# Differential attention on one core: heads that take turns, and band attention's output kept by token halves

## The chip, the cores and the metric

The kernel runs on one core of a Trainium2 chip. The metric is the device time of one execution in microseconds (us), the median of several runs. Engines are called PE (TensorE, the matrix engine; PEld is its weight load), DVE (VectorE), ACT (ScalarE), POOL (GpSimd) and SP (SyncE, which here only issues DMAs). Lnnn is a line of the kernel file before the change.

## The reference

One layer over 1024 tokens of width 1024, in float32: a SwiGLU feed-forward half step, two attentions in parallel whose gated outputs are added, and a second feed-forward half step. The part around the change, cut short:

```python
a = chunked_band_attention(qa, ka, va, rel_table)        # 8 heads of 64, band of 576 keys
b = diff_attention(qb, kb, vb, t5_table, lam, ...)       # 4 heads, see below
x = x + (sigmoid(g_a) * (a @ w_branch_a) + sigmoid(g_b) * (b @ w_branch_b)) @ w_o

# diff_attention, for a head h and a query block of 128 tokens (8 blocks):
sc   = q[r] @ k[r].T * scale + bias[h]                   # r = 0, 1: two score maps, d = 64
p    = softmax(where(allowed, sc, NEG))                  # keys up to the query's chunk
o    = (p[0] - lam * p[1]) @ v                           # v is 128 wide
y    = rms_norm(o, subln_g) * (1 - lambda_init)
```

Query block i sees the keys of blocks 0 to i, so block 0 has 128 keys and block 7 has 1024.

## The kernel before

Every product in float32 is made of three TensorE products of parts: a tensor is split into a rounded part (`whi`, cast on ACT, L96) and the remainder (`wlo`, subtracted on DVE, L101), and `mm3` issues hi·hi, lo·hi and hi·lo (L127, L128, L129).

The program runs through stages one after the other. By the timeline these are the first feed-forward block (to about 690 us), the norm and the projection into queries, keys, values and gates (to about 1112), band attention (to about 1225), differential attention (to about 1402), the gated sum with w_o (to about 1570) and the second feed-forward block. The change lies in band attention and in differential attention.

Both attentions are written as generators ("jobs"). `run(jobs)` keeps up to four jobs live and advances them in turn, the new one first. A job of differential attention, `jobs_b(hb, filler)`, is one query block of one head: it makes the two score maps on PE (`sc`, two PSUM banks), adds the bias `nb` and takes the minimum on DVE (L692, `pm`), takes the exponential on ACT (L694) and combines the two maps on DVE (L829). Then it rests for a turn. Then come the transposes of the probabilities on PE (L700, `pt`), split again on ACT and DVE (`whi`, `wlo`), the products with the values (L845 and L846, `pv`), the norm (`o`, `sq`, `dg`) and the final product `try` (L860), which is split into the output tile `y`. The jobs of a head run in the order of blocks 0 to 7, heads one after another.

With the first job of a head its operands are loaded from DRAM: six half tiles `qs`, `ks`, `kl` of 512 KB each (L123), two halves of 64 partitions apiece, and the values `vt` of 1024 KB. The bias `nb` (L705, two DMAs of 512 KB) serves two heads, so that it is loaded for the first and for the third head. Heads 0 to 3 of differential attention are called the first to the fourth here; their loads are `q4` to `q7` in the order below. A change of head is called a switch: switch 1 is from the first to the second head.

Between these jobs the kernel does a piece of other work, `branch_a`, in 16 filler steps: band attention's output times w_branch_a. A filler step reads a tile of gates `g` (`gl`), makes 12 matmuls into `pb`, multiplies on DVE (L794) and stores the result with a DMA on SP (`ta`, L795). After each block `due[0] += 0.5` says that half a step is due. One weight chunk `wa` (512 KB, L118, a single buffer) serves four filler steps, and each of its two column blocks is split once for two steps.

Nothing but the tile pools holds the loads back. The large tiles (8 KB per partition: `qs`, `ks`, `kl`, `vt`, `y`, `nb`) share the tag "big" with 14 buffers; units of split data have WU = 18 buffers, temporary tiles (`gl`, `o1`, `o2`, `sq` and others) TF = 10. The order of the instructions on each engine is set when the kernel is compiled, by a scheduler that works from the program order and from these pools. Each engine runs its instructions in that order, and all the DMAs named here are issued by SP in order: what waits on SP holds back what stands behind it.

Of the kernel before, what the change touches and what calls it, by code (L numbers as in the profile page):

```python
# [9 lines left out]
F32 = mybir.dt.float32  # L10
# [6 lines left out]
P = 128  # L17
S = 1024
D = 1024
NT = S // P  # L20
KT = D // P
HALF = 512
# [22 lines left out]
RAW, WU, TF, TT = 6, 18, 10, 3  # L45
# [8 lines left out]
def hybrid_layer_kernel(ctx, tc, x, ffn1_norm, ffn1_w_in, ffn1_w_out, mix_norm, w_mix_in,  # L54
# [13 lines left out]
    def big(shape, name, dtype=F32R):  # L68
        return sb.tile(shape, dtype, tag="big", bufs=14, name=name)
# [47 lines left out]
    def load(src, tile_):  # L117
        nc.sync.dma_start(out=tile_, in_=src)  # L118
        return tile_
# [535 lines left out]
    ys = []  # L655
    with tc.tile_pool(name="ps2", bufs=1, space=PSUM) as ps:
# [64 lines left out]
        def jobs_a(pr):  # L721
            ctx_ = {}

            def job(sb_, h):
                if not ctx_:
                    ctx_["qkv"] = load_qkv(pr)
                    ctx_["y"] = big([P, 2, S], "y")
                    ys.append(ctx_["y"])
                    ctx_["nb"] = big([P, 2, S], "nb", F32)
                    for hh in range(2):  # L730
                        bias_rows(ctx_["nb"][:, hh, :WA], diag_a, 2 * pr + hh, EA, WA)
                qkv, y, nb = (ctx_[n] for n in ("qkv", "y", "nb"))
# [66 lines left out]
        def jobs_b(hb, filler):  # L799
            ctx_ = {}  # L800

            def job(i):
                if not ctx_:
                    ctx_["qkv"] = load_qkv(4 + hb)
                    ctx_["y"] = big([P, 2, S], "y")
                    ys.append(ctx_["y"])
# [29 lines left out]
                due[0] += 0.5  # L836
# [32 lines left out]
        due = [0]  # L869
        for hb in range(4):  # L870
            jobs += jobs_b(hb, filler)
# [5 lines left out]
    with tc.tile_pool(name="ps3", bufs=1, space=PSUM) as ps:  # L877
# [7 lines left out]
        for jj in range(KT // 2):  # L885
            wr = load(w_cols(w_branch_b[0], jj * 256, 256, 0, 4), raw_tile([P, 4, 256]))
            for j in (2 * jj, 2 * jj + 1):
                w = split_units(wr[:, :, (j % 2) * P:(j % 2 + 1) * P], branch_unit)
                for g in range(2):
# [3 lines left out]
                    for k in range(4):  # L893
                        mm3(pb, [v[:, k, :] for v in w], [cols(ys[4 + k][:, v, :], g) for v in range(2)],
                            k == 0, k == 3)
# [83 lines left out]
```

## Time and profile before

| | |
|---|---|
| median of 3 runs | 2207.89 us (2207.6 to 2208.07) |
| profiled execution | 2210.82 us, its span 2209.0 us, mean PE clock 0.979 |
| PE busy in the span | 2100.4 us (95%) |
| DVE busy | 1448.2 us (66%) |
| ACT busy | 991.2 us (45%) |
| POOL busy | 286.4 us (13%) |
| differential attention, 1225 to 1402 us | PE 151.73 of 177, DVE 137.50, ACT 107.72 |

The profile has one execution. In a table by windows each row gives a stretch of time, its length, and the busy time of PE, PEld, DVE, ACT and POOL with the count of instructions in brackets; then the PE clock that was granted (1.00 is full), the mean busy share of the DMA engines and their rate in GB/s. In a timeline a row has the start, the duration, the engine, the line and what is written from what; a bracket at its end gives the idle time before it and what ended that.

### The profile page before, as it was taken

The numbers are of one execution on the slowest core, as the hardware profiler recorded it, in microseconds if no ns is written. First come the engines' busy times: TensorE is split into PE (matmuls) and PEld (weight loads), VectorE is DVE, ScalarE is ACT, GpSimd is POOL, SyncE is SP. The second block draws the span as 40 slices with busy tenths as digits, with TensorE's granted clock in tenths as the row PEclk, the third lists the DMA queues.
The fourth block names the chain that finished last, engine by engine and source line by source line (L and its number), as shares of the span: only waits on it lengthen the run. The fifth ranks groups of instructions, "written<-read, shape, count | busy, mean of one in ns | idle before, by whom it ended". The sixth has DMA issues, their size and how long they took to land. (4 is left out here: it accounts for less than half of the span.)

```text
span 2209.0 us, 29778 instructions
## 1 busy us (share of the span) xinstructions
PE 2100.4 (95%) x10373; PEld 1779.8 (81%) x10373; DVE 1448.2 (66%) x2620; ACT 991.2 (45%) x1972; POOL 286.4 (13%) x371
## 2 busy tenths in 40 slices
PE   5999999999997999999999988899799999999997
PEld 4888888888886998888878877788688888888886
DVE  8765656577567756655378877658756565658566
ACT  5433333334445444444478756335433333334444
POOL 6130000000006100000056333104300000000000
PEclk8999999999998999999999989999999999999999
DMA  4374323284353445542497555755423232367335
GB/s 136 100 198 115 119 83 118 96 305 162 115 154 112 134 154 171 172 148 91 120 226 184 125 152 139 225 166 172 119 86 120 88 116 93 111 224 240 97 115 186
DMA packets 262246, 319.72 MB, mean 145 GB/s; under 512 B 16732, under 2 KB 162156, under 8 KB 262096
## 3 DMA queue, kind: packets, MB, share of 16 engines
q1 hardware_dynamic: 257888, 309.91, 45.3%
q0 software_dynamic: 4064, 7.39, 1.5%
q8 instruction: 82, 1.34, 0.3%
q14 instruction: 68, 0.56, 0.1%
q10 hardware_dynamic: 144, 0.52, 0.1%
HBM read 219.44 MB, written 98.30 MB: 144 GB/s over the span
## 5 line engine op out<-in xcount | busy, mean ns | idle before, releaser
L101 DVE TENSOR_TENSOR wlo<-raw,whi 128x512 fp32r<-128x512 f32 x197 | 141.6, 719 | 183.3 <-PE prod L128 109.7
L96 ACT CAST whi<-raw 128x512 fp32r<-128x512 f32 x200 | 124.4, 622 | 273.8 <-PE prod L128 224.5
L96 ACT CAST whi<-T 128x512 fp32r<-128x512 f32 x192 | 119.5, 623 | 282.7 <-PE prod L128 163.0
L128 PE MATMUL po<-wlo,whi 128*128 128x512 f32 x616 | 240.0, 390 | 0.0
L129 PE MATMUL po<-whi,wlo 128*128 128x512 f32 x616 | 239.9, 390 | 0.0
L127 PE MATMUL po<-whi 128*128 128x512 f32 x616 | 236.4, 390 | 0.0
L101 DVE TENSOR_TENSOR wlo<-T,whi 128x512 fp32r<-128x512 f32 x189 | 134.2, 710 | 98.3 <-ACT whi L96 74.4
L112 DVE TENSOR_TENSOR c<-prod,c 128x512 f32<-128x512 f32 (+1 forms) x201 | 133.2, 664 | 99.7 <-PE prod L129 98.7
L101 DVE TENSOR_TENSOR wlo<-B,whi 128x512 fp32r<-128x512 f32 x154 | 107.0, 695 | 129.2 <-ACT whi L96 129.2
L96 ACT CAST whi<-B 128x512 fp32r<-128x512 f32 x154 | 95.7, 622 | 206.9 <-PE po L128 185.3
L138 POOL TENSOR_TENSOR r<-v,neg_half 128x1 f32<-128x1 f32 x64 | 44.3, 693 | 758.9 <-DVE v L155 721.2
L129 PEld LDWEIGHTS po<-whi,wlo 128*128 128x128 f32 x616 | 115.7, 188 | 24.1
L127 PEld LDWEIGHTS po<-whi 128*128 128x128 f32 x616 | 115.7, 188 | 23.9
L128 PEld LDWEIGHTS po<-wlo,whi 128*128 128x128 f32 x616 | 115.7, 188 | 23.8
L184 POOL TENSOR_TENSOR xt<-xt,gain 128x512 f32<-128x512 f32 x36 | 49.1, 1380 | 516.4 <-DMA xt<-xm 484.3
L96 ACT CAST whi<-ha 128x512 fp32r<-128x512 f32 x154 | 94.8, 616 | 39.0 <-PE prod L128 17.2
L101 DVE TENSOR_TENSOR wlo<-ha,whi 128x512 fp32r<-128x512 f32 x154 | 105.7, 687 | 10.0 <-ACT whi L96 10.0
L258 ACT COPY c<-prod 128x512 f32<-128x512 f32 (+1 forms) x201 | 103.3, 573 | 5.2 <-issue 2.6
L694 ACT ACTIVATE pm<-pm,mn 128x640 f32<-128x640 f32 (+7 forms) x128 | 94.1, 736 | 17.4 <-DVE mn L692 16.1
L127 PE MATMUL prod<-S1h,whi 128*128 128x512 f32 (+1 forms) x252 | 96.5, 383 | 2.2 <-ACT S1h L96 2.2
L127 PE MATMUL prod<-S4h,whi 128*128 128x512 f32 (+1 forms) x252 | 96.1, 381 | 1.8 <-ACT c L258 1.8
L127 PE MATMUL prod<-A11h,whi 128*128 128x512 f32 (+1 forms) x252 | 96.8, 384 | 0.7 <-ACT A11h L96 0.7
(247 smaller groups left out, 5835.4 us busy)
## 6 DMA issues: line engine op xcount, KB each, us to landing
raw<-in_ffn_w_in_dram SPq DMA_DIRECT2D x88, 512.0 KB, 3.9
ha<-hS SPq DMA_DIRECT2D x88, 256.0 KB, 2.7
raw<-in_w_mix_in_dram SPq DMA_DIRECT2D x40, 512.0 KB, 4.1
ha<-hA SPq DMA_DIRECT2D x66, 256.0 KB, 2.7
hA<-c SPq DMA_DIRECT2D x64, 256.0 KB, 2.5
B<-in_ffn_w_out_dram SPq DMA_DIRECT2D x12, 1024.0 KB, 5.9
hS<-hs SPq DMA_DIRECT2D x44, 256.0 KB, 2.1
hS<-c SPq DMA_DIRECT2D x42, 256.0 KB, 2.1
```

What stands on the lines that cost most here:

```text
L96: nc.scalar.copy(out=hi, in_=src)
L101: (nc.gpsimd if on_pool else nc.vector).tensor_tensor(out=lo, in0=src, in1=h, op=ALU.subtract)
L112: nc.vector.tensor_tensor(out=out_, in0=a, in1=b, op=op)
L127: nc.tensor.matmul(ps, a[0], b[0], start=first, stop=False, skip_group_check=shared)
L128: nc.tensor.matmul(ps, a[0], b[1], start=False, stop=False, skip_group_check=shared)
L129: nc.tensor.matmul(ps, a[1], b[0], start=False, stop=last, skip_group_check=shared)
L138: nc.gpsimd.tensor_tensor(out=r, in0=v, in1=neg_half, op=ALU.pow)
L184: (nc.vector if on_vector else nc.gpsimd).tensor_tensor(out=xt[h][d], in0=xt[h][d], in1=gain[:, c], op=ALU.mult)
L258: nc.scalar.copy(out=self.held[name], in_=p)
L694: nc.scalar.activation(out=dst, in_=dst, func=AF.Exp, bias=mn, scale=-1.0, accum_out=rs)
```

## The change

The first half of it concerns the order of the jobs. The first four blocks of the first head run as before; from there the last four blocks of a head take turns with the first four of the next: 4, 0', 5, 1', 6, 2', 7, 3'. The last four blocks of the fourth head stand alone.

The second half concerns the output of band attention. It was kept in one tile per pair of heads (`ys[0]` to `ys[3]`, each for all tokens); now it is kept in four tiles by token half and part (`y_a`, named `yah` and `yal`). `branch_a` runs over the token halves outermost. The first 8 filler steps need the first half alone, whose two tiles are free after them. For this each weight chunk `wa` is loaded twice (8 loads, where there were 4) and split twice (16 column blocks, where there were 8).

With it `due[0]` grows by 0.7 per block, so that the filler steps come closer together and are used up after block 23 of 32, and the pools change: 15 large buffers for 14, 16 units for 18, 8 temporary tiles for 10.

```diff
-RAW, WU, TF, TT = 6, 18, 10, 3
+RAW, WU, TF, TT = 6, 16, 8, 3
...
-        return sb.tile(shape, dtype, tag="big", bufs=14, name=name)
+        return sb.tile(shape, dtype, tag="big", bufs=15, name=name)
...
-                    ctx_["y"] = big([P, 2, S], "y")
-                    ys.append(ctx_["y"])
+                    if not y_a:
+                        y_a.extend([big([P, 4, HALF], f"ya{c}") for c in "hl"] for _ in range(2))
...
-                    c = slice(sb_ * 256, (sb_ + 1) * 256)
-                    split(ysum, y[:, 0, c], y[:, 1, c], on_pool=True)
+                    c = slice(sb_ % 2 * 256, (sb_ % 2 + 1) * 256)
+                    split(ysum, *(v[:, pr, c] for v in y_a[sb_ // 2]), on_pool=True)
...
         def branch_a():
-            for jj in range(KT // 2):
-                wr = load(w_cols(w_branch_a[0], jj * 256, 256, 0, 4), sb.tile([P, 4, 256], F32, tag="gain", bufs=1, name="wa"))
-                for j in (2 * jj, 2 * jj + 1):
-                    w = split_units(wr[:, :, (j % 2) * P:(j % 2 + 1) * P], branch_unit)
-                    for n in range(2):
-                        c = slice(n * HALF, (n + 1) * HALF)
+
+            for n in range(2):
+                c = slice(n * HALF, (n + 1) * HALF)
+                for jj in range(KT // 2):
+                    wr = load(w_cols(w_branch_a[0], jj * 256, 256, 0, 4),
+                              sb.tile([P, 4, 256], F32, tag="gain", bufs=1, name="wa"))
+                    for j in (2 * jj, 2 * jj + 1):
+                        w = split_units(wr[:, :, (j % 2) * P:(j % 2 + 1) * P], branch_unit)
                         gl = load(g_d[j][:, c], temp([P, HALF], "gl"))
                         pb = ps.tile([P, HALF], F32, tag="pv", bufs=2, name="pb")
                         for k in range(4):
-                            mm3(pb, [v[:, k, :] for v in w], [ys[k][:, v, c] for v in range(2)], k == 0, k == 3)
+                            mm3(pb, [v[:, k, :] for v in w], [v[:, k, :] for v in y_a[n]], k == 0, k == 3)
...
-                due[0] += 0.5
+                due[0] += 0.7
...
+        heads = [jobs_b(hb, filler) for hb in range(4)]
+        jobs += heads[0][:4]
         for hb in range(4):
-            jobs += jobs_b(hb, filler)
+            for i in range(4):
+                jobs += [heads[hb][4 + i]] + ([heads[hb + 1][i]] if hb < 3 else [])
```

While two heads are live the large buffers in use are four for `y_a`, two for the outputs of the two heads, one `nb` and twice four for `qs`, `ks`, `kl` and `vt`: 15.

**DVE at switch 1.** Rows of DVE in their order, before, around the first softmax of the second head (`sc_11951`; `sc_11849` and `sc_11859` are the two maps of the first head's last block):

```order
L692 ISA pm_11854,mn_11856<-sc_11849,nb_11409 128x1024
L692 ISA mn_11856 128x1
L829 SCALAR_TENSOR_TENSOR pm_11713<-pm_11723,ri_11729,pm_11713 128x768
L103 SCALAR_TENSOR_TENSOR y_11408<-try_11779,gsub_219,y_11408 128x128
L824 RECIPROCAL ri_11803<-rs_11789 128x1
L692 ISA pm_11864,mn_11866<-sc_11859,nb_11409 128x1024
...
L103 SCALAR_TENSOR_TENSOR y_11408<-try_11845,gsub_219,y_11408 128x128
L824 RECIPROCAL ri_11869<-rs_11855 128x1
L101 TENSOR_TENSOR wlo_11881<-pt_11875,whi_11880 128x512
L692 ISA pm_11954,mn_11956<-sc_11951,nb_11409 128x128
```

And with the change, up to the first softmax of the second head (`sc_11741`); five short rows ahead of these stands the product of the second filler step (`gl_11691`, called filler step 1, since the count begins at 0):

```order
L101 TENSOR_TENSOR wlo_11769<-pt_11763,whi_11768 128x512
L831 SCALAR_TENSOR_TENSOR pm_11658<-pm_11668,ri_11674,pm_11658 128x640
L856 ISA sq_11784,v_11785<-o1_11779 128x128
L856 ISA v_11785 128x1
L101 TENSOR_TENSOR wlo_11913<-wa_11836,whi_11912 128x512
L103 SCALAR_TENSOR_TENSOR y_11408<-try_11791,gsub_219,y_11408 128x128
L856 ISA sq_11873,v_11874<-o1_11868 128x128
L856 ISA v_11874 128x1
L101 TENSOR_TENSOR wlo_11827<-pt_11821,whi_11826 128x512
L101 TENSOR_TENSOR wlo_11833<-pt_11830,whi_11832 128x128
L103 SCALAR_TENSOR_TENSOR y_11408<-try_11880,gsub_219,y_11408 128x128
L692 ISA pm_11744,mn_11746<-sc_11741,nb_11409 128x128
```

The second head's first softmax moved from behind the first head's last and widest softmax to a place ahead of its block 5, close behind filler step 1.

**SP at switch 2.** The queue of DMAs before, at the loads of the third head (`q6`, `k6`):

```order
L118 DMA gl_12329<-g2_195 128x512
L123 DMA qs_12525<-q6_181 64x2x1024
L123 DMA ks_12526<-k6_189 64x2x1024
L123 DMA kl_12527<-k6_189 64x2x1024
L795 DMA ta2_211<-gl_12329 128x512
L123 DMA qs_12525<-q6_181 64x2x1024
L123 DMA ks_12526<-k6_189 64x2x1024
L123 DMA kl_12527<-k6_189 64x2x1024
L118 DMA wa_12788<-in_w_branch_a_dram 128x4x256
L123 DMA vt_12534<-v1_192 128x8x256
L705 DMA nb_12537<-diag_b_218 128x1024 x2
```

And with the change:

```order
L118 DMA gl_12149<-g5_198 128x512
L123 DMA kl_12340<-k6_189 64x2x1024
L123 DMA qs_12338<-q6_181 64x2x1024
L123 DMA ks_12339<-k6_189 64x2x1024
L123 DMA kl_12340<-k6_189 64x2x1024
L797 DMA ta5_214<-gl_12149 128x512
L118 DMA gl_12298<-g6_199 128x512
L118 DMA wa_12481<-in_w_branch_a_dram 128x4x256
L118 DMA gl_12390<-g7_200 128x512
L123 DMA vt_12347<-v1_192 128x8x256
L797 DMA ta6_215<-gl_12298 128x512
L705 DMA nb_12350<-diag_b_218 128x1024 x2
```

The store that stood between the two halves of the loads stands behind them now, and `vt` and `nb` moved further from the six half tiles, behind the loads for filler steps 6 and 7 and a store.

**PE at switch 2.** Matmuls before, at the first scores of the third head (`sc_12542`, `sc_12550`):

```order
L700 MATMUL pt_12404<-ident_66,pm_12244 128x128
L845 MATMUL pv_12498<-vt_11948,whi_12400 128x256
L684 MATMUL sc_12542<-ks_12526,qs_12525 128x128
L684 MATMUL sc_12550<-ks_12526,qs_12525 128x128
L860 MATMUL try_12431<-dg_12361,o1_12353 128x128
L846 MATMUL pv_12498<-vt_11948,wlo_12401 128x128
```

And with the change (`sc_12355`, `sc_12363`; `pb_12392` is filler step 7, the last that reads the first token half):

```order
L700 MATMUL pt_12283<-ident_66,pm_12107 128x128 x4
L684 MATMUL sc_12355<-ks_12339,qs_12338 128x128
L684 MATMUL sc_12363<-ks_12339,qs_12338 128x128
L685 MATMUL sc_12355<-kl_12340,qs_12338 128x128
L685 MATMUL sc_12363<-kl_12340,qs_12338 128x128
L127 MATMUL pb_12392<-yah_9632,whi_12386 128x512
L128 MATMUL pb_12392<-yal_9633,whi_12386 128x512
L129 MATMUL pb_12392<-yah_9632,wlo_12387 128x512
```

Filler step 7 stands behind the third head's first scores now. Of the 15 large buffers the third head's `qs`, `ks` and `kl` can take those of the first head's, after its last scores; its `vt`, its output and `nb` need three more, and those that come free next are the first head's `vt` and the two tiles of the first token half, which this filler step reads last.

More of the change, by code (lines that the diff above doesn't have):

```diff
@@ L731, in job @@
                         bias_rows(ctx_["nb"][:, hh, :WA], diag_a, 2 * pr + hh, EA, WA)
-                qkv, y, nb = (ctx_[n] for n in ("qkv", "y", "nb"))
+                qkv, nb = (ctx_[n] for n in ("qkv", "nb"))
                 vt = qkv[3]
@@ L893, in hybrid_layer_kernel @@
                     for k in range(4):
-                        mm3(pb, [v[:, k, :] for v in w], [cols(ys[4 + k][:, v, :], g) for v in range(2)],
+                        mm3(pb, [v[:, k, :] for v in w], [cols(y_b[k][:, v, :], g) for v in range(2)],
                             k == 0, k == 3)
```

4 lines of the change are left out of this document (2 added, 2 removed).

## The prediction

> **What bounds the kernel now.** I read the page first, then a table by windows over the stage that the change touches, then what PE waits for there, the chain of waits, and the queue of DMAs at the switches.
>
> ```profile
> span 2209.0 us, 29778 instructions
> PE 2100.4 (95%) x10373; PEld 1779.8 (81%) x10373; DVE 1448.2 (66%) x2620; ACT 991.2 (45%) x1972; POOL 286.4 (13%) x371
> ```
>
> Over the whole PE is the bound. By windows that holds for the feed-forward blocks and not for differential attention:
>
> ```profile
> 80.00:680.00 600.00, 599.71 (x2656) 496.67 (x2655) 380.13 (x598) 230.72 (x404) 27.76 (x53) 1.00 0.45 143
> ...
> 1225.00:1402.00 177.00, 151.73 (x906) 133.21 (x907) 137.50 (x429) 107.72 (x287) 56.35 (x101) 0.94 0.60 160
> ...
> 1600.00:2160.00 560.00, 559.71 (x2474) 463.62 (x2473) 353.69 (x557) 214.00 (x374) 0.00 (x0) 1.00 0.40 129
> ```
>
> So a gain can come only from the 177 us of differential attention, where PE has 25.3 us idle and DVE 39.5. Cut at the switches:
>
> ```profile
> 1225.00:1250.00 25.00, 24.69 (x148) 21.52 (x148) 24.44 (x76) 18.53 (x50) 5.77 (x11) 1.00 0.62 143
> 1250.00:1256.00 6.00, 3.98 (x32) 3.42 (x31) 4.59 (x18) 3.83 (x12) 2.33 (x4) 1.00 1.08 240
> 1256.00:1288.00 32.00, 30.67 (x192) 27.18 (x190) 27.71 (x88) 21.73 (x59) 10.74 (x20) 1.00 0.52 129
> 1288.00:1294.00 6.00, 0.91 (x6) 0.52 (x5) 4.08 (x11) 2.50 (x8) 2.56 (x4) 0.79 1.06 231
> 1294.00:1300.00 6.00, 4.89 (x22) 4.50 (x22) 1.10 (x4) 1.67 (x6) 0.11 (x1) 0.50 1.06 262
> 1300.00:1306.00 6.00, 5.95 (x26) 5.38 (x27) 3.76 (x13) 2.60 (x7) 2.81 (x5) 0.57 0.85 312
> 1306.00:1336.00 30.00, 28.76 (x174) 25.21 (x172) 26.18 (x84) 21.12 (x57) 8.66 (x18) 1.00 0.38 107
> 1336.00:1348.00 12.00, 5.44 (x26) 4.92 (x27) 4.11 (x18) 3.41 (x10) 2.33 (x4) 0.72 1.03 230
> 1348.00:1384.00 36.00, 34.02 (x214) 29.96 (x213) 31.91 (x99) 24.58 (x66) 14.45 (x24) 1.00 0.32 106
> 1384.00:1402.00 18.00, 12.43 (x80) 10.62 (x81) 9.61 (x26) 7.75 (x21) 6.58 (x12) 0.96 0.79 250
> ```
>
> Read DVE, the fifth number: it lacks 1.4 us of 6 at switch 1, 9.1 of 18 at switch 2 (three rows), 7.9 of 12 at switch 3 and 8.4 of 18 in the tail. The other 12.7 of the 39.5 us lie between, where DVE and PE are both nearly full. I keep the ledger on DVE, since each softmax passes it. At the switches the loads end the waits; the second and third rows below are steps of the chain, with start and length:
>
> ```profile
> PE sc L684 <- DMA ks<-k: 11.1, 2, 5.7
> 1245.40 9.51 DMA kl<-k
> 1283.61 11.23 DMA ks<-k
> 1294.88 0.69 PE L684 MATMUL sc<-ks,qs 128*128 128x128 f32 x2 [5.34 <-DMA ks<-k]
> 1342.40 0.66 PE L684 MATMUL sc<-ks,qs 128*128 128x128 f32 x2 [5.72 <-DMA ks<-k]
> ```
>
> **The change part by part.** The price of a head's loads, from the loads of the first head, which run in one go on an empty queue, and of the bias on a nearly empty one (issue times, then the landing, the last number of each row):
>
> ```profile
> 1185.55 0.58 SPq L123 DMA_DIRECT2D qs<-q  x1
> 1188.80 0.60 SPq L123 DMA_DIRECT2D kl<-k  x1
> kl<-k SPq DMA_DIRECT2D x1, 512.0 KB, 15.3
> nb<-diag_b SPq DMA_DIRECT2D x2, 512.0 KB, 7.4
> ```
>
> The last half tile lands 1188.80 + 15.3 − 1185.55 = 18.5 us after the first issue. Alternating the heads hides that only if PE and DVE have 18.5 us of other work between the issue and the first scores of the new head.
>
> *Switch 1.* The last four transfers of the second head stand on SP behind the store of filler step 1, before as after. Before:
>
> ```profile
> 1243.70 0.68 DVE L794 TENSOR_TENSOR gl<-pb,gl 128x512 f32<-128x512 f32 x1
> 1244.41 0.33 SPq L795 DMA_DIRECT2D ta<-gl  x1
> ```
>
> The first of these rows is DVE's product, the second the store behind it; then `kl` took 9.51 us to land. With the change I put the product's end at about 1240.6, an estimate: in DVE's order the rows from the start of the stage to it add up to 15.6 us at the durations of their forms. The store and four issues of 0.6 us follow, and `kl` lands near 1240.6 + 0.4 + 2.4 + 9.5 = 1253. DVE's order leaves between that product and the first softmax of the second head the twelve rows shown with the change and five short ones ahead of them: about 5 us, at durations like these:
>
> ```profile
> 1241.30 0.88 DVE L829 SCALAR_TENSOR_TENSOR pm<-pm,ri 128x640 f32<-128x640 f32 x1
> 1242.10 0.68 DVE L101 TENSOR_TENSOR wlo<-wa,whi 128x512 fp32r<-128x512 f32 x1
> 1242.70 1.08 DVE L692 CUSTOM_DVE_ANT_0 pm<-sc,nb 128x896 f32<-128x896 f32 x1
> ...
> 1244.44 0.33 DVE L103 SCALAR_TENSOR_TENSOR y<-try,gsub,y 128x128 fp32r<-128x128 f32 x1
> 1244.69 0.28 DVE L854 CUSTOM_DVE_ANT_0 sq<-o 128x128 f32<-128x128 f32 x1
> ```
>
> (0.88 + 3 × 0.68 + 3 × 0.33 + 3 × 0.28, and 0.3 for the smallest). Before, two softmaxes 1024 wide and much else stood there. So DVE is out of work at 1245.7 and waits to 1253: 7.5 us instead of 1.4, **+6.1**. It can be as low as 0, if the store goes out earlier than the order suggests.
>
> *Switch 2.* The six half tiles now go out in one row with no store between. In the order some 20 us of DVE's work lies between their release (the first head's last score) and the third head's first softmax, so DVE hides the 18.5 us; PE has 13.4 us of work there and stalls some 5 to 6 us. But filler step 7 stands behind those scores on PE, and the third head's `vt` and `nb` need the buffers that it frees. A filler step is 12 matmuls. The second and the ninth of one began at
>
> ```profile
> 1237.36 0.39 PE L128 MATMUL pb<-y,whi 128*128 128x512 f32 x1
> ...
> 1238.98 0.39 PE L129 MATMUL pb<-y,wlo 128*128 128x512 f32 x1
> ```
>
> so that one takes 12 × 1.62 / 7 = 2.8 us. Then `nb` takes at least 7.4 us, and 1 more for the `vt` ahead of it. Of these 11 us DVE covers 2.5. I take 9 us idle instead of 9.1: **0**. The worst is a landing like that of before in a full queue (13.3 us, the median of the two):
>
> ```profile
> nb<-diag_b SPq DMA_DIRECT2D x2, 512.0 KB, 13.3
> ```
>
> *Switch 3.* No bias is due. DVE has 16 us of work between release and first softmax against 18.5: 2.5 us idle instead of 7.9, **−5.4**, with a PE stall of about 6 us left.
>
> *Tail.* The fourth head's four wide blocks still run alone at the end, with no filler left: 7.5 for 8.4, **−0.9**. Without filler PE could also wait there more than now (the bound is +3).
>
> *Between the switches.* A wide block's softmax now stands beside a narrow block's short chain, and fillers come at 0.7 per block. Of the 12.7 us the change can take all or nothing; with no row nearer to one end I take the middle, **−6.4**.
>
> *The doubled weight chunks.* Eight further column blocks are split, each one cast on ACT and one subtraction on DVE:
>
> ```profile
> L101 DVE TENSOR_TENSOR wlo<-wa,whi 128x512 fp32r<-128x512 f32 x7 | 5.0, 718 | 0.5 <-PE pb L128 0.3
> L96 ACT CAST whi<-wa 128x512 fp32r<-128x512 f32 x6 | 3.8, 629 | 2.6 <-PE pb L129 2.4 <-DMA wa<-in_w_branch_a_dram 0.3
> ```
>
> On DVE that is 8 × 0.718 = 5.7 us, or 4.8 by the 0.60 us from start to start in the rows 1242.10 and 1242.70 above. I take **+4.8**, all on the path; those that fall into a wait cost nothing, so the bounds are 0 and 5.7. ACT, with 107.7 us of 177 busy, hides its 5.0. Four further `wa` loads of 512 KB are hidden where the DMA share is 0.3 to 0.5; at a switch, where it is over 1, they add about 2 us each, which I leave to the range.
>
> *Smaller pools.* With 16 units a split must wait for its unit sooner. Outside this stage ACT waits for a free unit all the time and yet runs ahead of PE:
>
> ```profile
> ACT whi L96 <- PE prod L128: 163.5, 92, 4.1
> PE prod L127 <- ACT c L258: 0.3, 1, 0.3
> ```
>
> (ACT in 80 to 680; PE in 1600 to 2160, its only wait.) Two units fewer take less than 1 us off a lead of nearly 4, and PE releases the units in any case; **0**, bounds −1 and +2. Eight temporary tiles do for all but a few moments: 0. The order of PE in the other stages is the same but for a few rows.
>
> *The clock.* After the stall of 5.34 us PE ran at 0.50 and 0.57 of its clock for two windows, after that of 5.72 at 0.72. While DVE sets the pace that costs little: 0 here, up to +3.4 in the range. The Trainium skill ("TensorE: Matmul & The Clock Gate", Part 1: The HAM clock gate) says that the clock halves after an idle window of about 3.4 us and is full again after about one busy window of the same length. The row of before agrees that a stall over 5 us halves it and not on the length, since 12 us passed at about half. By the page three stalls over 3.4 us would cost three ramps, one more than now; an estimate from it is 1.7 us more, and the sum would be −0.1 instead of −1.8.
>
> **The sum:** 6.1 + 0 − 5.4 − 0.9 − 6.4 + 4.8 = −1.8 us. The profiled execution took 2210.82 us, 2.93 above the median shown and 1.82 above its own span; it would become 2209.0. By the same difference the median of 2207.89 becomes 2206.1. I forecast 2206: no change that can be told. 0.2% is 4.4 us, about what a measurement of this kernel can tell from none.
>
> **The rivals.** *The loads are hidden after all* (faster). If the store of filler step 1 reaches SP some 6 us sooner, switch 1 stays at 1.4 us, and if `nb` lands within the work that DVE has, switch 2 falls from 9.1 to 2: 0 − 7.1 − 5.4 − 0.9 − 6.4 + 4.8 = −15.0, or 2193; with one of the two it is some −8, or 2200. For it: the share of DMA is 0.3 to 0.6 between switches, so the queue has room. Against it: the order of SP.
>
> *The bias comes late* (slower). The third head's `nb` waits for filler step 7, this for the third head's scores and these for its loads, all in a row. If `nb` then needs 13.3 us and not 7.4, DVE is idle 6 to 8 us longer, and the PE stall at half clock adds up to 3.4: −1.8 + 8 + 3.4 = +9.6, or 2217.5; 2213 with the smaller parts. It decides from a landing of 13.5 us after issue. For it: the landings shown from the switches took 9.5 to 13.3 us. Against: in the order few other transfers stand near.
>
> *The change does not do what it says.* All 15 buffers are taken while two heads are live, so that the loads could go out no sooner than now, with each switch at its old price and the mixing worth nothing: +4.8 less what the splits hide, 2208 to 2213.
>
> **How the numbers follow.** Forecast, 2201 to 2211: 0.42, of it 0.10 faster, 0.29 the same, 0.03 slower by over 0.2%. Loads hidden, 2190 to 2200: 0.25. Bias late, 2213 to 2222: 0.25. Does not do what it says: 0.08, of it 0.06 the same. That makes faster 0.35, same 0.35, slower 0.30. The range runs from 2195 to 2218; below it I leave 0.1 and above it 0.08.
>
> **What would show it.** Right: DVE idle 6 to 9 us ahead of the second head's first softmax, near 1246 to 1253, with `kl` landing last; the third head's scores with a PE stall of 4 to 7 us, and then DVE waiting for `nb` and not for scores; DVE idle under 4 us at switch 3; 16 subtractions of `wa`; the stage's end within 3 us of 1401. Wrong: no DVE wait over 3 us at switch 1 or 2 (then the first rival), a wait for `nb` of over 12 us (the second), or idle PE in the feed-forward blocks with ACT or DVE as releaser, which would be the smaller pools. The term that I trust least is that between the switches.

## The result and the profile after

The change made the kernel slower. The median of four runs is 2236.54 us (2234.84 to 2239.21) against 2207.98 for the kernel before on the same chip; the ratio is 1.0125 with a 95% interval of 1.0105 to 1.0144. The profiled execution took 2239.21 us, the slowest of the four. Two executions of about 7000 us in later measurements, one of them of the kernel before, are left out of the ratios.

```profile
span 2237.4 us, 29672 instructions
PE 2108.0 (94%) x10373; PEld 1782.3 (80%) x10373; DVE 1460.7 (65%) x2628; ACT 993.6 (44%) x1980; POOL 286.2 (13%) x371
```

The span grew by 28.4 us. I cut it at three events that both traces have: the first scores of band attention, the first scores of differential attention, and the last `try` of its last head. The windows between them, before (first fence) and after; the second number is the length:

```profile
1115.00:1218.20 103.20, 95.25 (x655) 83.82 (x656) 87.63 (x278) 89.43 (x230) 69.99 (x87) 0.97 0.86 198
1218.20:1400.40 182.20, 156.79 (x947) 137.47 (x945) 142.30 (x442) 112.80 (x299) 59.67 (x106) 0.94 0.57 152
```

```profile
1121.60:1237.60 116.00, 97.09 (x647) 85.85 (x647) 87.01 (x277) 88.95 (x229) 69.15 (x89) 0.93 0.77 177
1237.60:1428.80 191.20, 163.53 (x951) 139.71 (x951) 149.04 (x451) 117.27 (x308) 60.04 (x105) 0.95 0.56 157
```

So 6.6 us were lost ahead of band attention (it starts at 1121.6 for 1115.0), 12.8 in band attention and 9.0 in differential attention; what follows the last `try` took 808.6 us in both. Two of the three losses lie where I had expected none.

**Ahead of band attention.** ACT, PE and PE again, in time order:

```profile
158.72 1.07 ACT L258 COPY c<-prod 128x512 f32<-128x512 f32 x2 [9.33 <-DMA hA<-c]
159.36 0.79 PE L127 MATMUL prod<-S3h,whi 128*128 128x512 f32 x1 [5.03 <-ACT c L258]
716.12 2.05 PE L192 MATMUL tr<-dg,xt 128*128 128x128 f32 x8 [4.74 <-DVE A22l L101]
```

ACT waits 9.33 us for the store of an earlier temporary tile `c`: a temporary tile is missing, and PE stands still for 5.03 us. Before, PE had no wait of 1 us from 66 to 686 us. The longest wait of PE from 695 to 725 us was 2.19 us before. Idle PE in the feed-forward block with ACT as releaser is the sign that the prediction named for the smaller pools.

**In band attention.** POOL, then the engines that wait for it:

```profile
1178.89 0.40 POOL L750 TENSOR_TENSOR pm<-pm,ri 128x128 f32<-128x128 f32 x1
1191.58 0.14 POOL L707 MEMSET nb<- 64x64 f32 x1 [12.29 <-DMA nb<-diag_a]
...
1192.00 0.61 POOL L750 TENSOR_TENSOR pm<-pm,ri 128x256 f32<-128x256 f32 x1
1192.67 0.69 PE L700 MATMUL pt<-ident,pm 128*128 128x128 f32 x2 [8.83 <-POOL pm L750]
1194.56 0.82 DVE L692 CUSTOM_DVE_ANT_0 pm<-sc,nb 128x640 f32<-128x640 f32 x1 [9.45 <-POOL pm L750]
```

The fill of the edges of the *next* pair's bias (L707, L709) stands on POOL ahead of the *current* pair's normalizations (L750). It waits 12.29 us for that bias to land, POOL does nothing meanwhile, and PE and DVE run dry. The fills of the pair before this one and of the first bias of differential attention wait too, 4.93 and 5.68 us. Before, the same fill stood behind the last normalization of the pair and waited for nothing:

```profile
1191.99 1.25 POOL L750 TENSOR_TENSOR pm<-pm,ri 128x640 f32<-128x640 f32 x1
1197.47 0.73 POOL L101 TENSOR_TENSOR y<-ysum,y 128x256 fp32r<-128x256 f32 x1 [4.23 <-ACT y L96]
1198.15 0.14 POOL L707 MEMSET nb<- 64x64 f32 x1
```

**In differential attention.** DVE is the fifth number; these are switches 1, 2, 3 and the tail:

```profile
1262.00:1281.00 19.00, 11.89 (x54) 9.84 (x54) 7.44 (x26) 3.46 (x12) 4.87 (x8) 0.79 1.05 254
1307.00:1330.00 23.00, 18.27 (x108) 15.77 (x107) 13.29 (x39) 9.14 (x25) 6.58 (x14) 0.93 0.77 243
1352.00:1362.00 10.00, 7.42 (x43) 5.97 (x42) 6.61 (x20) 4.24 (x12) 1.56 (x4) 1.00 1.04 244
1400.00:1428.80 28.80, 23.13 (x151) 20.02 (x150) 23.05 (x67) 19.54 (x48) 12.00 (x23) 0.94 0.43 134
```

DVE is idle 11.6, 9.7, 3.4 and 5.8 us there, and 11.7 in between: 42.2 against 39.9 in the whole stage before. Its work grew by 6.7 us, 5.5 of it in 15 subtractions of `wa` for 7 within the stage. At switch 1 one wait is 7.02 us; `kl`, issued at 1264.70, had landed at 1277.8, 13.1 us later. At switch 2 the 9.7 us are several waits; the two longest and the one ahead of the first softmax are shown last:

```profile
1278.33 0.29 DVE L692 CUSTOM_DVE_ANT_0 pm<-sc,nb 128x128 f32<-128x128 f32 x1 [7.02 <-PE sc L685]
...
1314.22 0.69 DVE L796 TENSOR_TENSOR gl<-pb,gl 128x512 f32<-128x512 f32 x1 [2.75 <-DMA gl<-g]
1317.80 0.69 DVE L101 TENSOR_TENSOR wlo<-wa,whi 128x512 fp32r<-128x512 f32 x1 [2.89 <-PE pb L128]
1325.37 0.29 DVE L692 CUSTOM_DVE_ANT_0 pm<-sc,nb 128x128 f32<-128x128 f32 x1 [1.17 <-POOL nb L707]
```

### The profile page after: what moved, and what is told of

Same layout as the page of the kernel before. It is cut to its first block, busy times and chain, and to the rows that moved or that the text cites. A ratio compares the mean times of both kernels' runs of the same rounds, so it can differ in the third digit from the quotient of the medians.

```text
span 2237.4 us, 29672 instructions
## 1 busy us (share of the span) xinstructions
PE 2108.0 (94%) x10373; PEld 1782.3 (80%) x10373; DVE 1460.7 (65%) x2628; ACT 993.6 (44%) x1980; POOL 286.2 (13%) x371
## 4 chain that ended last, share of the span: by engine, by line
PE 38%; DMA 5%; DVE 3%; issue 2%; ACT 1%; POOL 1%; SPq 0%; DVEq 0%; POOLq 0%; ACTq 0%
PE prod L129 6%; PE prod L127 6%; PE prod L128 6%; PE po L127 4%; PE po L128 4%; PE po L129 4%; DMA kl<-k 1%; PE pb L127 1%; DVE pm L692 1%; DMA nb<-diag_b 1%; PE pb L128 1%; DMA gl<-g 1%; PE pb L129 1%; DMA qs<-q 1%; DVE wlo L101 1%
## 5 line engine op out<-in xcount | busy, mean ns | idle before, releaser
L692 DVE CUSTOM_DVE_ANT_0 pm<-sc,nb 128x640 f32<-128x640 f32 (+7 forms) x128 | 88.1, 698 | 36.0 <-PE sc L685 15.3
L127 PE MATMUL prod<-S3h,whi 128*128 128x512 f32 (+1 forms) x252 | 96.7, 384 | 5.4 <-ACT c L258 5.4
L192 PE MATMUL tr<-dg,xt 128*128 128x128 f32 x320 | 51.5, 321 | 50.8 <-DVE A22l L101 19.9
```

Source lines behind the costliest of these rows:

```text
L127: nc.tensor.matmul(ps, a[0], b[0], start=first, stop=False, skip_group_check=shared)
L192: nc.tensor.matmul(tr[:, k, :], xt[h][d][:, k * P:(k + 1) * P], diag[h], start=True, stop=True)
L692: nc.vector.tensor_tensor_reduce(out=d3, in0=sc, in1=nb.rearrange("p (n w) -> p n w", n=n), scale=1.0, scalar=3e38, op0=ALU.add, op1=ALU.m ...
```

## The experiments

All ratios below are to the kernel before on the same chip. The stage columns come from one profile each, and runs of one kernel spread by 2 to 12 us, so that a stage is good to a few us only (an estimate) and the ratio is the judge. Heads "in turn" come one after another, with half a filler step per block as before unless a row says otherwise; so do those of the run with y by halves only.

| run | ratio (95%) | band attention starts | band | differential |
|---|---|---|---|---|
| before | 1 | 1115.0 | 103.2 | 182.2 |
| changed | 1.0125 (1.0105 to 1.0144) | 1121.6 | 116.0 | 191.2 |
| pools only | 1.0024 (1.0014 to 1.0033) | 1121.2 | 101.4 | 179.9 |
| temporary tiles only | 1.0024 (1.0013 to 1.0036) | 1117.5 | 102.3 | 183.0 |
| y by halves only | 1.0051 (1.0036 to 1.0065) | 1114.8 | 108.8 | 186.1 |
| changed, heads in turn | 1.0114 (1.0097 to 1.0131) | 1122.3 | 116.2 | 188.5 |
| the same, fillers by chunk | 1.0128 (1.0111 to 1.0145) | 1125.4 | 115.3 | 189.6 |
| changed, both biases' edges free | 1.0076 (1.0061 to 1.0091) | 1120.3 | 98.9 | 195.6 |
| before, the same | 1.0050 (1.0035 to 1.0065) | 1113.8 | 104.4 | 194.2 |
| changed, band's edges free | 1.0092 (1.0076 to 1.0109) | 1122.6 | 103.8 | 193.4 |
| changed, stores on ACT | 1.0131 (1.0114 to 1.0148) | 1122.6 | 116.7 | 191.9 |
| before, stores on ACT | 0.9972 (0.9963 to 0.9981) | 1115.0 | 102.3 | 178.4 |
| changed, stores and chunks on ACT | 1.0119 (1.0100 to 1.0139) | 1121.3 | 114.2 | 185.9 |
| changed, mended | 1.0022 (1.0013 to 1.0031) | 1114.3 | 102.8 | 188.5 |
| before, mended | 0.9983 (0.9973 to 0.9992) | 1113.3 | 100.7 | 177.5 |
| changed, all mended | 1.0019 (1.0010 to 1.0029) | 1115.4 | 103.0 | 187.0 |
| all mended, fillers spread | 1.0019 (1.0007 to 1.0030) | 1114.2 | 102.6 | 187.4 |
| all mended, heads in turn | 0.9958 (0.9947 to 0.9970) | 1115.5 | 102.6 | 173.2 |
| the same, pace 0.7 | 1.0014 (1.0005 to 1.0024) | 1114.6 | 101.2 | 190.7 |
| the same, old pools | 0.9982 (0.9970 to 0.9994) | 1113.7 | 104.0 | 184.0 |

**The pools alone.** The kernel before with the three sizes of the change.

```diff
-RAW, WU, TF, TT = 6, 18, 10, 3      # and bufs=14
+RAW, WU, TF, TT = 6, 16, 8, 3       # and bufs=15
```

> The kernel before with the three pool sizes of the change alone (15 large buffers, 16 units, 8 temporary tiles); order of the heads, y and filler steps as before. Theory A: the 15th large buffer lets the scheduler put the loads of the next pair's bias, and with them the fills of its edges on POOL (L707, L709), ahead of the current pair's normalizations (L750); POOL then waits for the bias to land and everything behind it waits too. By A band attention is 8 to 13 us longer than before (first scores of differential attention less first scores of band attention: 103.3 us before, 116.0 changed). Theory B: 8 temporary tiles make the feed-forward blocks wait (5 us near 159 us in the changed kernel). A and B together: 2219 to 2227 us. Rival: the loss of band attention comes from y_a holding four large buffers from the start; then band attention stays at 103 to 105 us here and the total at 2208 to 2214.

Theory A fell in the cause that it named: with the 15th buffer and without y by halves, band attention is as short as before.

```profile
1121.20:1222.60 101.40, 92.87 (x656) 81.10 (x656) 87.44 (x278) 89.72 (x230) 70.14 (x87) 1.00 0.90 202
```

Theory B held: the waits near 159 us (4.23 us) and 716 us (4.69) are here, and the total is 1.0024, 2215.8 us, below the 2219 to 2227 that A and B together would have given. Which pool it is:

```diff
-RAW, WU, TF, TT = 6, 18, 10, 3
+RAW, WU, TF, TT = 6, 18, 8, 3
```

> The kernel before with 8 temporary tiles for 10 and nothing else. The three pool sizes together cost about 6 us ahead of band attention (1115.0 to 1121.2 us), with one wait of ACT for a temporary tile near 159 us (4 to 5 us on PE) and one of 4.7 us near 716. If the temporary tiles are the cause of both: band attention starts near 1121 and the total is 2213 to 2216. If the units are: it starts at 1115 and the total is that of before within 2 us. One wait each: 1118 and about 2212.

The same ratio, with ACT waiting for the same store:

```profile
158.63 0.59 ACT L258 COPY c<-prod 128x512 f32<-128x512 f32 x1 [9.09 <-DMA hA<-c]
```

PE waits 2.52 us there, and band attention starts at 1117.5 and not at 1121. The wait near 716 us was absent in this profile, so it takes more than the temporary tiles: it is in every profile with 16 units and 8 tiles. It was absent too in the mended runs below, which have 14 units, 10 temporary tiles and 15 large buffers and start band attention at 1114 to 1116. So fewer units cost nothing where there are ten tiles; with eight they may add to it, though the two ratios do not differ.

**The heads in turn again**, and y by halves alone.

```diff
-        jobs += heads[0][:4]
         for hb in range(4):
-            for i in range(4):
-                jobs += [heads[hb][4 + i]] + ([heads[hb + 1][i]] if hb < 3 else [])
+            jobs += heads[hb]              # and due[0] += 0.5
```

> The changed kernel with the heads one after another again and 0.5 of a filler step per block; y by token halves, doubled weight chunks and the new pool sizes stay. If the alternation itself costs the 9 us that differential attention lost (182.1 to 191.2 us), the total falls by about 9 to 2227, with band attention still at 116 us. If those 9 us are the doubled weight chunks (4.8 on DVE) and what else y by halves brings, differential attention stays at 187 us or more and the total at 2232 or above. If the alternation were the cause of everything: 2208 to 2213.

> The kernel before with y_a by token halves and the filler steps over token halves, the doubled weight chunks with it; order of the heads, 0.5 of a step per block and pool sizes as before. Theory A2: y_a alone takes the room that made the next pair's bias wait, so the fills of its edges stand earlier on POOL and stop it. Then band attention starts at 1115 and takes 112 to 117 us, differential attention 186 to 190 (the doubled chunks), total 2226 to 2232. Rival: only y_a together with the 15th buffer does it; then band attention takes 103 to 106 and the total is 2213 to 2219.

Without the alternation, and at the old pace of the fillers, the changed kernel is as slow as with them: the intervals overlap. The alternation, the part that I had spent my sum on, did nothing here that the ratio can tell. y by halves alone costs 0.5%, on both sides of the start of differential attention, and y by halves with the new pools 1.1%. The rival of the second run (only both together) is half right: y by halves alone stops POOL for less, since its fills stand less far ahead: 12 to 14 rows of POOL earlier than before, where they stand 16 or 17 earlier with the new pools.

```profile
1215.66 0.55 PE L700 MATMUL pt<-ident,pm 128*128 128x128 f32 x3 [2.71 <-POOL pm L750]
```

**Is it the fill on POOL?** Each bias is loaded in two DMAs that leave out the edges, so that the fills need not wait for it. The form for band attention's biases, cut short (that of differential attention has the first edge alone):

```diff
-nc.sync.dma_start(out=dst, in_=<128 rows of w>)
-nc.gpsimd.memset(dst[:64, w - 64:], BIG)
-nc.gpsimd.memset(dst[64:, :64], BIG)
+nc.gpsimd.memset(dst[:64, w - 64:], BIG)
+nc.gpsimd.memset(dst[64:, :64], BIG)
+nc.sync.dma_start(out=dst[:64, :w - 64], in_=<64 rows>)
+nc.sync.dma_start(out=dst[64:, 64:], in_=<64 rows>)
```

> The changed kernel, but each bias tile is loaded in two DMAs of 64 partitions that leave out the edges, and POOL fills the edges ahead of them, so that the fills wait for no bias. Theory A: POOL no longer waits in band attention, the stage falls from 116.0 to 103 to 106 us, the total to about 2224. Rival: the bias itself lands late because the queue is full, and the softmax waits for it where POOL waited; then the stage stays above 112 us and the total at 2233 or more.

> The kernel before with the same edit of the bias loads, as a control. Before, POOL's fills stood behind the normalizations of the pair and waited for nothing there. Theory A: no change beyond 3 us, 2205 to 2210. If the smaller DMAs are dearer: up to 2214.

> The changed kernel; only the biases of band attention are loaded without their edges, so that POOL's fills wait for no bias there; the bias of differential attention is loaded as in the changed kernel. In the run that did it for both, band attention fell from 116.0 to 98.9 us but differential attention rose from 191.2 to 195.6, as in the control (182.1 to 194). If the smaller loads of the second bias were the reason: band attention 99 to 101, differential attention 188 to 192, total 2217 to 2222. If the early start of differential attention itself cost the time (its loads waiting for buffers all the same): differential attention stays at 195 and the total at 2225 or more.

Yes, as a mechanism: POOL waits for no bias of band attention any more, and the stage fell from 116.0 to 98.9 and, with the edit for band attention's biases alone, to 103.8 us; in the latter POOL still waits 5.92 us for the second bias. The total fell by less (1.0076 and 1.0092 for 1.0125): differential attention took 2 to 4 us longer. Whether its earlier start is the reason was not settled.

The control missed its forecast (2205 to 2210 expected, 2221.1 measured): differential attention took 12 us longer. I had put that down to the smaller loads of the second bias, and the third run missed the forecast made from it (2217 to 2222 expected, 2230.1 measured): its differential attention stayed at 193.4 without those loads. The control's profile has more than half of the loss at switch 1, where no bias is loaded. A weight chunk stands ahead of the second head's loads on SP, and PE waits 7.62 us where it waited 1.2 at most before:

```profile
1237.88 0.38 SPq L118 DMA_DIRECT2D wa<-in_w_branch_a_dram  x1
1238.36 0.61 SPq L123 DMA_DIRECT2D qs<-q  x1
...
1256.88 0.66 PE L684 MATMUL sc<-ks,qs 128*128 128x128 f32 x2 [7.62 <-issue]
```

So the edit moved the order on SP as well, and the smaller loads are not shown to be the cause.

**Is it the doubled chunks?** The heads in turn, the filler steps by chunk as before, on top of y by halves.

```diff
-            for n in range(2):
-                for jj in range(KT // 2):
-                    ...
+            for jj in range(KT // 2):
+                ...
+                    for n in range(2):
```

> The run with the heads one after another (2236.3 us; differential attention 188.6), but with the filler steps in the old order, so that each weight chunk is loaded and split once (4 loads, 8 column blocks); y_a and the new pool sizes stay. If the doubled chunks are what differential attention lost: 188.6 falls to 180 to 183 and the total to 2228 to 2231. If it is the later start and the queue at the switches: it stays at 187 or more, the total above 2234. Band attention stays at 116 in both.

No. Eight subtractions, 5.4 us, went (DVE is busy 143.85 us for 148.13) and the stage stayed at 189.6. Less work on DVE alone does not shorten this stage. At switch 1 a chunk stands ahead of the second head's loads here too, though each is loaded once; in the kernel before it stood behind them. This run first, then before:

```profile
1264.94 0.38 SPq L118 DMA_DIRECT2D wa<-in_w_branch_a_dram  x1
1265.41 0.58 SPq L123 DMA_DIRECT2D qs<-q  x1
```

```profile
1246.12 0.54 SPq L123 DMA_DIRECT2D vt<-v  x1
1246.70 1.39 SPq L118 DMA_DIRECT2D wa<-in_w_branch_a_dram  x1
```

**The stores and the loads on SP.** The queue at switch 1 in the changed kernel:

```profile
1255.35 0.38 SPq L118 DMA_DIRECT2D wa<-in_w_branch_a_dram  x1
1255.95 0.33 SPq L797 DMA_DIRECT2D ta<-gl  x1
1256.38 0.38 SPq L118 DMA_DIRECT2D gl<-g  x1
1256.85 0.59 SPq L123 DMA_DIRECT2D qs<-q  x1
...
1262.39 0.33 SPq L797 DMA_DIRECT2D ta<-gl  x1
1262.77 0.58 SPq L123 DMA_DIRECT2D kl<-k  x1
```

```diff
-                        nc.sync.dma_start(out=ta_d[j][:, c], in_=gl)
+                        nc.scalar.dma_start(out=ta_d[j][:, c], in_=gl)
```

> The changed kernel with one edit: the stores of the filler steps (ta) are issued by ACT and not by SP, so that no store stands ahead of a head's loads. Theory C: at switch 1 of the changed kernel five of seven loads stood behind the store of filler step 1 on SP (1262.39 us, loads behind it from 1262.77) and kl landed at 1277.8; without it all loads go out with the first ones near 1257 and switch 1's idle DVE falls from 11.6 to 5 or 6 us; differential attention 191.2 to 183 to 187, total 2229 to 2233. Rival: the loads wait for their buffers anyway (released by the first head's scores); then the stage stays at 190 or more and the total at 2235 to 2238, or above if ACT now waits for DVE's product.

> The kernel before with the same edit. In it two half tiles of the second head and three of the third stood behind a store. Theory C: switches 1 and 2 shorten by 2 to 6 us together, total 2201 to 2206. Rival: unchanged within 2 us, since the loads of the third and fourth head start when the head before has made its last scores.

In the kernel before it is a gain of 0.28%: the second head's first load leaves at 1220.01 and not at 1234.83.

```profile
1220.01 0.58 SPq L123 DMA_DIRECT2D qs<-q  x1
```

In the changed kernel it is none. There the loads still leave at 1258, since the second chunk stands ahead of them too:

```profile
1257.06 0.38 SPq L118 DMA_DIRECT2D wa<-in_w_branch_a_dram  x1
1257.54 0.46 SPq L118 DMA_DIRECT2D gl<-g  x1
1258.08 0.59 SPq L123 DMA_DIRECT2D qs<-q  x1
```

That load waits until the first chunk's two blocks are split, for `wa` has a single buffer. With the chunks on ACT's queue as well:

```diff
-                    wr = load(w_cols(...), sb.tile(..., tag="gain", bufs=1, name="wa"))
+                    wr = sb.tile(..., tag="gain", bufs=1, name="wa")
+                    nc.scalar.dma_start(out=wr, in_=w_cols(...))
```

> The run of the changed kernel with the stores on ACT (2239.9 us, differential attention 191.9), with the weight chunks wa loaded by ACT's queue too. Theory D: on SP the second chunk, which waits for the buffer of the first, stood ahead of the second head's loads; without it these leave 2 to 6 us after the start of the stage instead of 19, switch 1 has no wait, and differential attention takes 180 to 186 us, total 2228 to 2234 with band attention still at 116. Rival: the large buffers are what the loads wait for; then they leave as late as before and the stage stays at 190 or more, total 2238 or more.

Theory D holds for the mechanism, in part. Four of the six half tiles leave from 1233.54 on, ahead of the stage's start, PE waits for no load at switch 1 any more, and the profile has 185.9 us for the stage. But that profile is the fastest of its four executions; the median, 2237.0, missed the forecast (2228 to 2234), and the interval overlaps that of the run without the edit.

The last two half tiles leave at 1257.43 and 1258.11. What SP waited for, here and in the kernel before with its stores on ACT (one row each: total, count, longest):

```profile
SPq L123 <- DMA wa<-in_w_branch_a_dram: 21.3, 1, 21.3
```

```profile
SPq L123 <- DMA ta<-gl: 13.1, 1, 13.1
```

These are the chunk and the store that ACT had issued: the load and the transfer that it waits for have one completion semaphore in the trace, and the load leaves within 0.1 us of the landing. So another queue frees the loads only in part, and the tile pools are not all that holds them back.

**The mends together.** Band attention's edges free, stores on ACT, 10 temporary tiles and 14 units; then the chunks on ACT as well. The second is the control on the kernel before, with its own pools.

> The changed kernel with three mends: bias edges of band attention free of the bias loads (band 116 to 104 us), stores on ACT, and 10 temporary tiles again, paid for with 14 units for 16. If the temporary tiles alone made the feed-forward wait, band attention starts at 1115 to 1118; with the other two the total is 2212 to 2220. If fewer units cost as much: start at 1120 or later, total 2222 or more. If the alternation of heads is worth what it was meant for, this is where it shows: differential attention under 180 us and the total under 2210.

> The kernel before with bias edges of band attention free and stores on ACT: the candidate for the fastest, and the control for the run above without the alternation, y by halves and the new pools. Band attention 100 to 104 us, differential attention 176 to 182, total 2199 to 2207. If it is no faster than before (2208 to 2210), neither the fills nor the stores cost the kernel before anything.

> The mended changed kernel (2214.8 us, differential attention 188.5) with the weight chunks on ACT as well. Theory D: differential attention 176 to 182, total 2203 to 2208. Rival, as above: 2214 or more.

The feed-forward and band attention are back to their old times, and some 24 of the 28 us with them. Differential attention is not: 188.5 and 187.0 us. The control on the kernel before lies in its forecast range with 2206.2 us and is no faster than with the stores on ACT alone. So I took the alternation out of the last changed kernel:

> The same with the heads one after another and 0.5 of a step per block: what the alternation is worth when the bias, the stores and the chunks are out of its way. If the alternation hides the loads at the switches, this is 4 to 10 us slower than the run above. If the loads leave early anyway, nothing is left to hide at switch 1 and only switches 2 and 3 differ: 0 to 4 us. If alternating costs (narrow blocks later, all buffers full): this run is the faster one.

```profile
1218.50:1405.50 187.00, 165.13 (x952) 142.01 (x952) 148.95 (x451) 117.90 (x307) 61.58 (x105) 0.94 0.57 158
```

```profile
1218.10:1391.30 173.20, 153.70 (x951) 134.53 (x951) 146.94 (x451) 117.49 (x308) 65.03 (x106) 0.99 0.62 175
```

With the heads in turn the stage takes 13.8 us less (2200.8 for 2213.9 us in the medians), DVE is idle 26.3 for 38.0 us, and PE runs at 0.99 of its clock for 0.94. The last half tile of the second head lands at 1247.2 in turn and 1247.7 alternating, that of the fourth at 1335.0 and 1334.7. So with early loads the alternation and its pace, which were taken out together, hide nothing more and cost 13 us. Two more runs asked whether that is the order of the blocks or the pace of the fillers, which the alternation needs, since the third head's buffers wait for filler step 7:

```diff
-                due[0] += 0.7
+                due[0] += 0.7 if due[1] < 8 else 0.4     # alternating; due[1] counts the steps taken
```

> The alternating run with all mends (2213.9 us, differential attention 187.0), with 0.7 of a filler step per block for the first 8 steps and 0.4 from there, so that the steps last to the end. If the pace is the cause: differential attention 174 to 179 and total 2201 to 2206. If the order of the blocks is: 184 to 188, total 2211 to 2215.

```diff
-                due[0] += 0.5
+                due[0] += 0.7                            # heads in turn
```

> The run with the heads in turn and all mends (2200.8 us, differential attention 173.2), with 0.7 of a filler step per block for 0.5. If the pace is the cause: differential attention 180 to 187, total 2208 to 2215. If the order of the blocks is: 172 to 176, total 2200 to 2204.

Neither answer is clean. The pace of 0.7 alone costs the run in turn the whole 12 us (2213.2), so pace is enough for the loss; but spreading the second half of the steps does not give the alternating run anything back, so there the pace of the first half or the order of the blocks is the cause. Alternating at 0.5 throughout was not tried, because the third head would need buffers that are not yet free. In the run in turn at 0.7 PE waits ahead of a filler step, which in the other runs of this stage is at most 1.4 us:

```profile
1294.06 0.77 PE L127 MATMUL pb<-yah,whi 128*128 128x512 f32 x1 [5.53 <-ACT pm L694]
```

The last run put 14 large buffers and 18 units back into the fastest version.

> The run with the heads in turn and all mends, with the pool sizes of before for two of the three pools that still differ (14 large buffers, 18 units; 10 temporary tiles as there): the kernel before with y by halves and the mends alone. If the 15th large buffer is what let the loads leave early: differential attention 177 or more and total 2205 or more. If not: the same within 3 us, 2198 to 2204.

2207.2 us; its runs spread from 2200 to 2212. Its interval begins where that of 15 buffers and 14 units ends (0.9970), so those sizes are probably worth something to the heads in turn, 0.24% by the ratios. Two pools were changed at once, so that the 15th buffer is not shown to be the one.

**The fastest version** is the changed kernel with all mends and the heads in turn: 2200.81 us (2196.61 to 2206.15), ratio 0.9958. The kernel before with nothing but the stores on ACT has 2203.26 us and 0.9972; their intervals overlap.

## Why the prediction was wrong

I forecast 2206 us, within 2195 to 2218; it was 2236.5.

*The bound.* "So a gain can come only from the 177 us of differential attention" was right for gains. I let it stand for losses as well, and 19.4 of the 28.4 us were lost outside.

*The step that failed first: band attention at nothing.* The change writes band attention's output into other tiles, and I costed that part at zero on the ground that PE's order was the same there. POOL's order was not: the fills of the next bias stand up to 17 rows earlier in it. The stage grew by 12.8 us, of which 12.2 went again with the fills freed of the loads, and no term of the sum or rival held them.

*The smaller pools, 0 with bounds −1 and +2.* They cost some 5 us, outside the bounds. The temporary tiles, passed over with "for all but a few moments", met one such moment at 159 us and PE stood for 5 us. The units, for which I gave a reason, cost nothing beside ten tiles; beside eight that stays open. The reason was weak: the 4.1 us that I took for ACT's lead are the longest of its 92 waits, whose mean is 1.8.

*Switch 1, +6.1.* The wait that `kl` ended is 7.02 us where I had 7.5; with the smaller waits beside it the window has 11.6 us idle, 10.2 more than the 1.4 of before. The path was the one described (SP, then `kl`), but the gate was not only the store: a weight chunk stands ahead of the loads, which the runs with stores and chunks on ACT showed. `kl` took 13.1 us to land and not 9.5. So the nearness of 7.02 to 7.5 is in part luck.

*Switch 2, 0, and switch 3, −5.4.* 9.7 us for 9 and 3.4 for 2.5: the sizes are right. At switch 3 the path is too: one wait of 3.0 us for the scores. At switch 2 it is so only in part, and the size is partly luck: 1.2 us of the 9.7 end on the bias, the rest on the filler steps' gates and products and on smaller things, and PE waited 3.7 us for the loads and not 5 to 6. The rival of the late bias did not come: the DMAs of `nb` landed 6.3 and 8.4 us after issue.

*Tail, −0.9.* 5.8 us idle for 7.5: a little better than said.

*Between the switches, −6.4.* 11.7 us against 12.7: the mixing gave nothing. This term had no row behind it, and taking the middle of its bounds turned a forecast loss of 4.6 us into a gain of 1.8.

*The doubled splits, +4.8.* The work came as counted (5.5 us), but taking it away gave nothing back. As a price on the path the term is not borne out. What a chunk did cost is its place in SP's queue ahead of a head's loads: 6 us of the stage in the profiles with and without it there (191.9 and 185.9), though the totals do not tell the two apart. For that it need not be loaded twice: the run with the fillers by chunk and the control of the bias edges have it there too.

*The rivals.* That the loads are hidden came near to true only in the mended runs, and even there the alternation with its pace lost: at switches 1 and 3 the loads land as early without it.

## What to carry to other kernels

Compare the order of every engine in every stage whose tiles or pools a change touches, the small ones first: here a fill of 0.14 us that waited 12.29 us for a DMA stopped POOL and all that stood behind it. Before hiding a load behind other work, look what stands ahead of it in its queue, and whether it waits for a transfer of another queue; in the kernel before, moving sixteen stores to ACT gained 0.28%, while the new order of the jobs gained nothing in any pair of runs. A term without a row of its own should not decide the sign of a sum.

## What the runs showed of the hardware

The clock of PE fell without a long stall. In the alternating run with all mends, at switch 3, in windows of 3 us:

```profile
1328.00:1331.00 3.00, 2.46 (x11) 1.69 (x9) 2.54 (x10) 0.82 (x3) 1.28 (x2) 1.00 1.02 199
1331.00:1334.00 3.00, 1.33 (x10) 1.10 (x10) 0.00 (x0) 0.59 (x1) 0.00 (x0) 0.97 1.03 223
1334.00:1337.00 3.00, 2.09 (x6) 1.91 (x7) 1.11 (x5) 1.35 (x5) 0.00 (x0) 0.50 1.09 355
1337.00:1340.00 3.00, 2.38 (x9) 2.08 (x8) 1.71 (x4) 0.37 (x1) 0.00 (x0) 0.50 0.88 305
1340.00:1343.00 3.00, 3.00 (x15) 3.00 (x15) 1.95 (x4) 1.79 (x4) 0.45 (x1) 0.50 0.41 158
1343.00:1346.00 3.00, 3.00 (x19) 2.82 (x18) 2.82 (x11) 2.50 (x7) 1.28 (x2) 0.82 0.32 108
```

```profile
1331.26 0.44 PE L684 MATMUL sc<-ks,qs 128*128 128x128 f32 x2 [0.80 <-DMA ks<-k]
1331.54 1.06 PE L700 MATMUL pt<-ident,pm 128*128 128x128 f32 x8
1334.73 0.69 PE L685 MATMUL sc<-kl,qs 128*128 128x128 f32 x2 [2.13 <-DMA kl<-k]
```

The longest wait is 2.13 us, yet three windows of 3 us run at half clock and a part of the fourth: ten short matmuls between two waits, eight of them transposes, did not keep it up. Whether it is their number or their kind, no run shows. The Trainium skill ("TensorE: Matmul & The Clock Gate", Part 1: The HAM clock gate) has the clock halve after an idle window of about 3.4 us; this run agrees only if a window with some short matmuls in it counts as idle. Over the stage the heads in turn had 0.99 of the clock for 0.94, and PE was busy 153.70 us for 165.13; how much of their gain the clock is, and how much the shorter waits that kept it up, was not taken apart.
